# A 90-degree rotation of an 8192 x 8192 float32 matrix: the last output split into a 448-row and a 576-row part

## The chip, the cores and the metric

The kernel runs on one core of one Trainium2 chip. The metric is the device time in microseconds (us) of one execution; the median of several is given. Beside it stands a profile of one execution. Engines are named as in the profile: PE (TensorE, with PEld for its weight loads), DVE (VectorE), ACT (ScalarE), POOL (GpSimd) and SP (SyncE). SP and ACT also issue the transfers between HBM and SBUF, which 16 DMA engines carry out.

## The reference

```python
def setup_inputs():
    return {"x": np.random.randn(8192, 8192).astype(np.float32), "k": 1}

def reference(x, k):
    return np.rot90(x, k)
```

With k = 1, out[i, j] = x[j, 8191 - i]: the matrix is transposed, and the order of its columns is reversed on the way. No arithmetic is done; 268 MB are read and 268 MB are written.

## The kernel before

The matrix is cut into 16 macro blocks (`macros`) of 1024 rows (`R`) by 4096 columns (`W`), numbered `kk`. A block is read in eight loads of 128 rows by 4096 columns (2 MB; `T` = 8 loads, number `t` in the block). Each row of a load lies in a partition of its own as 16 KB. A block gives eight outputs of 2 MB (`J` = 8, number `j`), each of 512 columns of x (`CH`), that is 512 rows of the output, by 1024 columns of the output. All loads come through five buffers `buf0` to `buf4` (`LAND` + `OUTS`, 16 KB in each partition), which also hold the outputs before they are stored.

Four engines work in a chain, each with its own hand-written order.

- SP issues the loads (L160), each as soon as the buffer that it needs has been emptied (the wait at L190). At the end it waits until all stores have landed (L195).
- DVE copies each loaded buffer into `ring`, which has 63 slots of 512 columns, and reverses each 512-column chunk on the way (L209). The copy is cut into pieces where a ring slot is set free late (`pieces`, L120 to 140). The semaphore `s_rev` counts the pieces.
- PE transposes 128 x 128 blocks of `ring` by a matmul with an identity matrix into PSUM (L241). PSUM is split in two halves `ps0` and `ps1` of 2048 elements in each partition; `s_half` says that a half is full.
- ACT copies the halves into an output buffer (L272, 128 x 2048 each; `s_ev`), waits for the second one, and issues the store (L277). The store's semaphore is that of its buffer, `s_store`. Before the first half is copied, the earlier store from the same buffer must have landed (L265 to 270).

The list `outs` (L70 to 74) gives the outputs in order. Those of the first 15 blocks take one `j` and all eight `t`. The last block is taken differently: four `t` and two `j` at a time (512 columns of the output by 1024 of its rows), so the first four outputs need `t` = 0 to 3 alone; where `js` starts at 0, PE goes by `t` first (L250). The last output of all is `(15, range(4, 8), range(6, 8))`: j = 7 in the first half of PSUM, j = 6 in the second, four blocks of 128 rows each. In the store, each of the 128 partitions holds eight runs of 512 elements (2 KB), one for each block of 128 rows of the output. `out_buf` (L109) names the buffer of each output; in the last block it goes round all five.

`LINE` and `HEAD` (L28, L29) set where the buffers start in SBUF: `head` is padded so that all five start at a multiple of 1024 bytes. `whole_reads` rewrites the read side of the loads so that a row is read as one run.

The functions that the change touches, with the line numbers of the profile:

Of the kernel before, what the change touches and what calls it, by code (L numbers as in the profile page):

```python
# [6 lines left out]
P = 128  # L7
# [5 lines left out]
G = 4  # L13
J = W // (G * P)
# [3 lines left out]
CH = G * P  # L18
F = G * R
SLOTS = T * J - 1  # L20

END = T // 2

H = 2
LAND = 2
OUTS = 3

LINE = 1024  # L28
HEAD = 224  # L29


def whole_reads(nc):
# [17 lines left out]
def slot(kk, t, j):  # L50

    at = t * J + j if kk % 2 == 0 else J + t + j * T
    return (at + kk // 2 * (J + 1)) % SLOTS


def kernel(tc: tile.TileContext, x: bass.AP, k: bass.AP, out: bass.AP):
    nc = tc.nc
# [3 lines left out]
    N, M = x.shape  # L61
    dt = x.dtype
    macros = [(r0, c0) for r0 in range(0, N, R) for c0 in range(0, M, W)]
    KK = len(macros)
    n_out = KK * J
# [4 lines left out]
    outs = [(kk, range(T), [j]) for kk in range(KK - 1) for j in range(J)]  # L70
    wide = T // END
    for t in range(0, T, END):
        for j in range(0, J, wide):
            outs.append((KK - 1, range(t, t + END), range(j, j + wide)))
    assert len(outs) == n_out


    order = [(kk, a, b) for kk in range(KK) for a in range(T) for b in range(J)]
# [5 lines left out]
    with tc.tile_critical():  # L84
        head = nc.alloc_sbuf_tensor("head", [P, HEAD], dt)
        ident, scratch = head[:, :P], head[:, P : P + 1]
        bufs = [nc.alloc_sbuf_tensor(f"buf{i}", [P, F], dt) for i in range(LAND + OUTS)]
        ring = nc.alloc_sbuf_tensor("ring", [P, SLOTS * CH], dt)
        for b in bufs:
            assert nc.lookup_mloc(b).addr % LINE == 0  # L90
        ps = [
# [8 lines left out]
        s_first = nc.alloc_semaphore("s_first")  # L100
        s_half = nc.alloc_semaphore("s_half")
        s_ev = nc.alloc_semaphore("s_ev")

        def load_buf(m):
            if m < T:
# [1 line left out]
            return LAND + 2 if m == T else (m - T - 1) % LAND  # L107

        def out_buf(n):  # L109
            e = n - (n_out - J)  # L110
            if e < 0:
                return LAND + (n + 1) % OUTS
            ends = [load_buf(n_load - 2)]
            ends += [LAND + (n_out - J + i + 1) % OUTS for i in range(OUTS)]
            ends += [load_buf(n_load - 1)]
            return ends[e % len(ends)]

# [24 lines left out]
        def runs(kk, t, lo, hi):  # L142

            at = [slot(kk, t, j) for j in range(lo, hi)]
            i = 0
            while i < len(at):
                n = 1
                step = at[i + 1] - at[i] if i + 1 < len(at) else 1
                if step > 0:
                    while i + n < len(at) and at[i + n] - at[i + n - 1] == step:  # L150
                        n += 1
                else:
                    step = 1
                yield lo + i, n, at[i], step
                i += n

        def load(e, m):
            r0, c0 = macros[m // T]
            b = load_buf(m)
            e.dma_start(  # L160
                out=bufs[b][:], in_=x[r0 + m % T * P : r0 + (m % T + 1) * P, c0 : c0 + W]
            ).then_inc(s_land[b], 16)

        def uses_before(n_or_m, buf):
            return sum(buf(i) == buf(n_or_m) for i in range(n_or_m))
# [4 lines left out]
        with nc.Block() as block:  # L170

            @block.gpsimd
            def _(e):
                e.memset(ident, 0.0).then_inc(s_id, 1)  # L174
                e.wait_ge(s_id, 1)
                e.affine_select(  # L176
                    out=ident,
                    in_=ident,
                    compare_op=mybir.AluOpType.not_equal,
                    fill=1.0,  # L180
                    base=0,
                    pattern=[[-1, P]],
                    channel_multiplier=1,
                ).then_inc(s_id, 1)

            @block.sync
            def _(e):
                for m in range(LAND + OUTS, n_load):
                    last = [i for i in range(m) if load_buf(i) == load_buf(m)]
                    e.wait_ge(s_rev, rev[last[-1], J - 1])  # L190
                    load(e, m)
                for b in range(LAND + OUTS):
                    n = sum(out_buf(i) == b for i in range(n_out))
                    if n:
                        e.wait_ge(s_store[b], 16 * n)  # L195

            @block.vector
            def _(e):
                for m in range(n_load):
                    kk, t = divmod(m, T)  # L200
                    b = load_buf(m)
                    a = bufs[b][:].rearrange("p (j c) -> p j c", c=CH)
                    e.wait_ge(s_land[b], 16 * (uses_before(m, load_buf) + 1))
                    for lo, hi, wait in pieces[m]:
                        if wait:
                            e.wait_ge(*wait)
                        for j, n, at, step in runs(kk, t, lo, hi):
                            v = ring[:, at * CH : (at + (n - 1) * step + 1) * CH]
                            i = e.tensor_copy(  # L209
                                out=bass.AP(  # L210
                                    tensor=v.tensor,
                                    offset=v.offset,
                                    ap=[v.ap[0], [step * CH, n], [1, CH]],
                                ),
                                in_=a[:, j : j + n, ::-1],
                            )
                        i.then_inc(s_rev, 1)

            @block.tensor
            def _(e):  # L220
                seen = {}

                def wait(sem, n):
                    if seen.get(sem, 0) < n:
                        seen[sem] = n
                        e.wait_ge(sem, n)

                e.wait_ge(s_id, 2)
                for n, (kk, ts, js) in enumerate(outs):
                    blocks = [(j, g) for j in reversed(js) for g in range(G)]  # L230
                    half = len(blocks) // H
                    rows = len(ts) * P

                    def transpose(t, b):
                        j, g = blocks[b]
                        if n:
                            wait(s_ev, H * (n - 1) + b // half + 1)
                        wait(s_rev, rev[kk * T + t, j])
                        at = slot(kk, t, j) * CH + g * P
                        f = b % half * rows + (t - ts[0]) * P  # L240
                        i = e.transpose(  # L241
                            ps[b // half][:, f : f + P], ring[:, at : at + P], ident
                        )
                        if t == ts[-1] and b % half == half - 1:
                            i.then_inc(s_half, 1)
                        elif t == ts[0] and b == len(blocks) - 1:
                            i.then_inc(s_first, 1)

                    order = [(t, b) for b in range(len(blocks)) for t in ts]
                    if js[0] == 0:  # L250
                        order.sort()
                    for t, b in order:
                        transpose(t, b)

            @block.scalar
            def _(e):
                e.wait_ge(s_id, 2)
                e.copy(scratch, ident[:, :1])  # L258
                for n, (kk, ts, js) in enumerate(outs):
                    r0, c0 = macros[kk]  # L260
                    rows = len(ts) * P
                    b = out_buf(n)
                    for h in range(H):
                        if h == 0:
                            stores = uses_before(n, out_buf)  # L265
                            loads = [i for i in range(n_load) if load_buf(i) == b]
                            if stores:
                                e.wait_ge(s_store[b], 16 * stores)
                            elif loads:
                                e.wait_ge(s_rev, rev[loads[-1], J - 1])  # L270
                        e.wait_ge(s_half, H * n + h + 1)  # L271
                        e.copy(  # L272
                            bufs[b][:, h * F // H : (h + 1) * F // H], ps[h][:]
                        ).then_inc(s_ev, 1)
                    top = M - c0 - (js[-1] + 1) * CH
                    e.wait_ge(s_ev, H * (n + 1))
                    e.dma_start(  # L277
                        out=out[
                            top : top + len(js) * CH, r0 + ts[0] * P : r0 + ts[0] * P + rows
                        ].rearrange("(g m) f -> m g f", m=P),  # L280
                        in_=bufs[b][:].rearrange("m (g f) -> m g f", f=rows),
                    ).then_inc(s_store[b], 16)


# [33 lines left out]
```

## Time and profile before

| | |
|---|---|
| time, median of 3 runs | 1265.5 us (1265.28 to 1265.51) |
| time of the profiled execution | 1265.5 us |
| its span, first to last instruction | 1263.6 us |
| PE busy | 693.0 us (55%) |
| DVE busy | 402.9 us (32%) |
| ACT busy | 467.0 us (37%) |
| moved by DMA | 537 MB, mean 425 GB/s over the span |
| load: issue to landing, median | 16.8 us |
| store: issue to landing, median | 25.7 us |
| last store issued by ACT | at 1246.11 us, taking 1.17 us |

The span counts from the first to the last instruction of the program; the execution's own time is 1.9 us longer. "Busy" is the time in which an engine works, as a share of the span; the rows by line give the number of instructions, the mean time of one, and what ended the idle time before it. A stretch of the profile is given as start:end in us from the span's start. In its rows the DMA share is the mean busy share of the 16 DMA engines, and GB/s is what they moved. A transfer has a time of issue, on the engine that issues it, and a landing, when all of its bytes have arrived; the trace marks the end of each DMA engine's share of it apart.

### The profile page before, as it was taken

The numbers are of one execution on the slowest core, as the hardware profiler recorded it, in microseconds if no ns is written. First come the engines' busy times: TensorE is split into PE (matmuls) and PEld (weight loads), VectorE is DVE, ScalarE is ACT, GpSimd is POOL, SyncE is SP. The second block draws the span as 40 slices with busy tenths as digits, with TensorE's granted clock in tenths as the row PEclk, the third lists the DMA queues.
The fourth block names the chain that finished last, engine by engine and source line by source line (L and its number), as shares of the span: only waits on it lengthen the run. The fifth ranks groups of instructions, "written<-read, shape, count | busy, mean of one in ns | idle before, by whom it ended". The sixth has DMA issues, their size and how long they took to land.

```text
span 1263.6 us, 9359 instructions
## 1 busy us (share of the span) xinstructions
PE 693.0 (55%) x4096; PEld 647.0 (51%) x4096; DVE 402.9 (32%) x313; ACT 467.0 (37%) x258; POOL 0.7 (0%) x6
## 2 busy tenths in 40 slices
PE   1556554665545655566555555555555555556563
PEld 1445454555545545565554554555445554455563
DVE  3323432234323343322342233422234222442210
ACT  0344333433344333433334333343333433434363
POOL 0000000000000000000000000000000000000000
PEclk9987767677677776767767777777776777767787
DMA  9999999999999999999999999999999999999998
GB/s 398 415 429 429 431 426 429 428 430 429 429 428 429 429 428 429 429 428 429 428 430 428 428 429 429 429 429 428 429 429 429 429 430 427 430 429 429 428 421 338
DMA packets 36904, 537.48 MB, mean 425 GB/s; under 512 B 4096, under 2 KB 4096, under 8 KB 4096
## 3 DMA queue, kind: packets, MB, share of 16 engines
q10 hardware_dynamic: 18432, 268.44, 50.0%
q1 hardware_dynamic: 18432, 268.44, 49.8%
q8 instruction: 32, 0.52, 0.2%
q14 instruction: 8, 0.07, 0.0%
HBM read 268.44 MB, written 268.44 MB: 425 GB/s over the span
## 4 chain that ended last, share of the span: by engine, by line
DMA 80%; issue 7%; ACT 5%; DVE 5%; PE 2%; ACTq 0%; SPq 0%
DMA buf<-in_x_dram 64%; DMA out_dram<-buf 16%; ACT buf L272 5%; DVE ring L209 5%; PE ps L241 2%; ACTq L277 0%; ACTq L271 0%; SPq L313 0%; SPq L84 0%
## 5 line engine op out<-in xcount | busy, mean ns | idle before, releaser
L241 PE MATMUL ps<-head,ring 128*128 128x128 f32 x4096 | 693.0, 346 | 550.7 <-ACT buf L272 472.8
L241 PEld LDWEIGHTS ps<-head,ring 128*128 128x128 f32 x4096 | 647.0, 184 | 596.5 <-ACT buf L272 511.5
L272 ACT COPY buf<-ps 128x2048 f32<-128x2048 f32 x256 | 465.5, 1870 | 778.2 <-DMA out_dram<-buf 594.8
L209 DVE COPY ring<-buf 128x512 f32<-128x512 f32 (+7 forms) x313 | 402.9, 1336 | 812.1 <-DMA buf<-in_x_dram 811.7
L258 ACT ACT_TABLE_LOAD x1 | 1.3, 1283 | 0.9 <-SPq L84 0.9
L176 POOL TENSOR_SCALAR_AFFINE_SELECT head<-head 128x128 f32<-128x128 f32 x1 | 0.3, 293 | 0.2 <-POOL head L174 0.2
L174 POOL MEMSET head<- 128x128 f32 x1 | 0.2, 204 | 0.5 <-SPq L84 0.5
L258 ACT COPY head<-head 128x1 f32<-128x1 f32 x1 | 0.2, 191 | 0.0
L299 POOL MEMSET const-bfloat16-1.0<- 128x1 bf16 x1 | 0.1, 101 | 0.0
L299 POOL MEMSET const-uint8-127<- 128x1 uint8 x1 | 0.1, 101 | 0.0
L299 POOL MEMSET const-float32-0.0<- 128x1 f32 x1 | 0.1, 98 | 0.2 <-issue 0.2
L299 POOL MEMSET const-float32-1.0<- 128x1 f32 x1 | 0.1, 98 | 0.0
## 6 DMA issues: line engine op xcount, KB each, us to landing
buf<-in_x_dram SPq DMA_DIRECT2D x128, 2048.0 KB, 16.8
out_dram<-buf ACTq DMA_DIRECT2D x128, 2048.0 KB, 25.7
```

Of the source, the lines that this page charges most:

```text
L174: e.memset(ident, 0.0).then_inc(s_id, 1)
L176: e.affine_select(out=ident, in_=ident, compare_op=mybir.AluOpType.not_equal, fill=1.0, base=0, pattern=[[-1, P]], channel_multiplier=1,). ...
L209: i = e.tensor_copy(out=bass.AP(tensor=v.tensor, offset=v.offset, ap=[v.ap[0], [step * CH, n], [1, CH]],), in_=a[:, j : j + n, ::-1],)
L241: i = e.transpose(ps[b // half][:, f : f + P], ring[:, at : at + P], ident)
L258: e.copy(scratch, ident[:, :1])
L272: e.copy(bufs[b][:, h * F // H : (h + 1) * F // H], ps[h][:]).then_inc(s_ev, 1)
L299: nc = _bacc.Bacc("TRN2", target_bir_lowering=False, num_devices=1)
```

## The change

The last output is popped off the list and replaced by two. Rows of the output are counted from the top of the 1024 rows that the old one covered: 512 rows for j = 7, then 512 for j = 6.

- The first new output (`n_few`) holds 448 of the 512 columns of the chunk j = 7. DVE writes them into the ring slot as 16 groups of 28, each in a place of 32 columns, in an order that goes with the store. PE transposes 64 of these columns at a time, so that 28 rows of the output come to partitions 0-27 and 28 to partitions 32-59; the four partitions after each hold nothing that is stored. ACT copies two halves of 64 x 2048 as before and issues no store. SP, behind its last load, waits for the second half and issues eight stores: for each of the two partition ranges four (`SPLIT`), each of seven partitions that lie four apart, with eight runs of 512 elements in each partition. All count on a new semaphore, `s_few`.
- The second new output holds the 512 rows of j = 6 in the first half of PSUM, as before, and the remaining 64 columns of the chunk j = 7 in the second half, transposed from a new tensor `extra` (256 elements in each partition) as four blocks of 64 columns. ACT copies 128 x 2048 and 64 x 512 and issues two stores: four blocks of 128 rows, and one block of 64 rows, the latter counted on `s_few`.
- For the four loads t = 4 to 7 of the last block, DVE's piece for j = 7 becomes two copies: the 448 columns to the ring and the 64 to `extra`.
- `extra` needs room: `HEAD` shrinks from 224 to 160 and `LINE` from 1024 to 256, so that the buffers and the ring start elsewhere.
- SP's final waits take in `s_few`.

The stores and transposes of all other outputs are as they were. The core of the diff:

```diff
@@ -25,8 +25,12 @@
 
-LINE = 1024
-HEAD = 224
+FEW = 28
+SPLIT = 4
+EIGHTH = 32
+
+LINE = 256
+HEAD = 160
 
@@ -73,6 +77,21 @@
     assert len(outs) == n_out
+    kk, ts, js = outs.pop()
+    ends = [js[-1], js[0]]
+    assert len(js) == 2 and END * P * H * G == F
+    few = [(ends[0], i * 2 * FEW, FEW) for i in range(H * G)]
+    rest = [(ends[0], H * G * 2 * FEW, CH - H * G * 2 * FEW)]
+    outs.append((kk, ts, js, [few[:G], few[G:]]))
+    outs.append((kk, ts, js, [[(ends[1], g * P, P) for g in range(G)], rest]))
+    n_out += 1
+    n_few = n_out - 2
+
+    def halves(n):
+        if len(outs[n]) == 4:
+            return outs[n][3]
+        blocks = [(j, g * P, P) for j in reversed(outs[n][2]) for g in range(G)]
+        return [blocks[: len(blocks) // H], blocks[len(blocks) // H :]]
 
@@ -86,6 +105,7 @@
         ring = nc.alloc_sbuf_tensor("ring", [P, SLOTS * CH], dt)
+        extra = nc.alloc_sbuf_tensor("extra", [P, END * (CH - H * G * 2 * FEW)], dt)
         for b in bufs:
@@ -100,6 +120,7 @@
         s_ev = nc.alloc_semaphore("s_ev")
+        s_few = nc.alloc_semaphore("s_few")
 
@@ -107,11 +128,11 @@
         def out_buf(n):
-            e = n - (n_out - J)
+            e = n - (KK * J - J)
             if e < 0:
                 return LAND + (n + 1) % OUTS
             ends = [load_buf(n_load - 2)]
-            ends += [LAND + (n_out - J + i + 1) % OUTS for i in range(OUTS)]
+            ends += [LAND + (KK * J - J + i + 1) % OUTS for i in range(OUTS)]
             ends += [load_buf(n_load - 1)]
@@ -189,8 +210,28 @@
                     load(e, m)
+                kk, ts, js, _ = outs[n_few]
+                b = out_buf(n_few)
+                top = M - macros[kk][1] - (js[-1] + 1) * CH
+                left = macros[kk][0] + ts[0] * P
+                rows = len(ts) * P
+                e.wait_ge(s_ev, H * (n_few + 1))
+                for at in (0, EIGHTH):
+                    for d in range(SPLIT):
+                        first = top + at // EIGHTH * FEW + d
+                        e.dma_start(
+                            out=bass.AP(
+                                tensor=out.tensor,
+                                offset=out[first : first + 1, left : left + 1].offset,
+                                ap=[[SPLIT * M, FEW // SPLIT], [2 * FEW * M, H * G], [1, rows]],
+                            ),
+                            in_=bufs[b][at + d : at + FEW : SPLIT].rearrange(
+                                "m (g f) -> m g f", f=rows
+                            ),
+                        ).then_inc(s_few, 16)
+                e.wait_ge(s_few, 16 * (2 * SPLIT + 1))
                 for b in range(LAND + OUTS):
-                    n = sum(out_buf(i) == b for i in range(n_out))
+                    n = sum(out_buf(i) == b and i != n_few for i in range(n_out))
                     if n:
@@ -204,6 +245,21 @@
                             e.wait_ge(*wait)
+                        if kk == KK - 1 and t >= END and lo == J - 1:
+                            v = ring[:, slot(kk, t, lo) * CH :][:, :CH]
+                            i = e.tensor_copy(
+                                out=v.rearrange("p (g c) -> p g c", c=EIGHTH)[:, :, :FEW],
+                                in_=a[:, lo, CH - H * G * 2 * FEW :].rearrange(
+                                    "p (g c) -> p g c", c=FEW
+                                )[:, ::-1, ::-1],
+                            )
+                            width = CH - H * G * 2 * FEW
+                            i = e.tensor_copy(
+                                out=extra[:, (t - END) * width : (t - END + 1) * width],
+                                in_=a[:, lo, width - 1 :: -1],
+                            )
+                            i.then_inc(s_rev, 1)
+                            continue
                         for j, n, at, step in runs(kk, t, lo, hi):
@@ -226,60 +282,80 @@
                 e.wait_ge(s_id, 2)
-                for n, (kk, ts, js) in enumerate(outs):
-                    blocks = [(j, g) for j in reversed(js) for g in range(G)]
-                    half = len(blocks) // H
+                for n, (kk, ts, js, *_) in enumerate(outs):
+                    parts = halves(n)
                     rows = len(ts) * P
 
-                    def transpose(t, b):
-                        j, g = blocks[b]
+                    def transpose(t, h, b):
+                        j, off, width = parts[h][b]
                         if n:
-                            wait(s_ev, H * (n - 1) + b // half + 1)
+                            wait(s_ev, H * (n - 1) + h + 1)
                         wait(s_rev, rev[kk * T + t, j])
-                        at = slot(kk, t, j) * CH + g * P
-                        f = b % half * rows + (t - ts[0]) * P
-                        i = e.transpose(
-                            ps[b // half][:, f : f + P], ring[:, at : at + P], ident
-                        )
-                        if t == ts[-1] and b % half == half - 1:
+                        at = slot(kk, t, j) * CH + off
+                        f = b * rows + (t - ts[0]) * P
+                        v = ring[:, at : at + width]
+                        if n == n_few:
+                            width = 2 * EIGHTH
+                            at = slot(kk, t, j) * CH + b * width + h * G * width
+                            v = ring[:, at : at + width]
+                        elif n > n_few and h:
+                            at = (t - ts[0]) * width
+                            v = extra[:, at : at + width]
+                        i = e.transpose(ps[h][:width, f : f + P], v, ident)
+                        if t == ts[-1] and b == len(parts[h]) - 1:
                             i.then_inc(s_half, 1)
-                        elif t == ts[0] and b == len(blocks) - 1:
+                        elif t == ts[0] and h == H - 1 and b == len(parts[h]) - 1:
                             i.then_inc(s_first, 1)
 
-                    order = [(t, b) for b in range(len(blocks)) for t in ts]
+                    order = [
+                        (t, h, b) for h in range(H) for b in range(len(parts[h])) for t in ts
+                    ]
                     if js[0] == 0:
                         order.sort()
-                    for t, b in order:
-                        transpose(t, b)
+                    for t, h, b in order:
+                        transpose(t, h, b)
 
             @block.scalar
             def _(e):
                 e.wait_ge(s_id, 2)
                 e.copy(scratch, ident[:, :1])
-                for n, (kk, ts, js) in enumerate(outs):
+                for n, (kk, ts, js, *_) in enumerate(outs):
                     r0, c0 = macros[kk]
+                    parts = halves(n)
                     rows = len(ts) * P
                     b = out_buf(n)
                     for h in range(H):
                         if h == 0:
-                            stores = uses_before(n, out_buf)
+                            before = uses_before(n, out_buf)
                             loads = [i for i in range(n_load) if load_buf(i) == b]
-                            if stores:
-                                e.wait_ge(s_store[b], 16 * stores)
+                            if before:
+                                e.wait_ge(s_store[b], 16 * before)
                             elif loads:
                                 e.wait_ge(s_rev, rev[loads[-1], J - 1])
                         e.wait_ge(s_half, H * n + h + 1)
+                        width = 2 * EIGHTH if n == n_few else parts[h][0][2]
+                        f = len(parts[h]) * rows
                         e.copy(
-                            bufs[b][:, h * F // H : (h + 1) * F // H], ps[h][:]
+                            bufs[b][:width, h * F // H : h * F // H + f], ps[h][:width, :f]
                         ).then_inc(s_ev, 1)
+                    if n == n_few:
+                        continue
                     top = M - c0 - (js[-1] + 1) * CH
+                    col = r0 + ts[0] * P
                     e.wait_ge(s_ev, H * (n + 1))
-                    e.dma_start(
-                        out=out[
-                            top : top + len(js) * CH, r0 + ts[0] * P : r0 + ts[0] * P + rows
-                        ].rearrange("(g m) f -> m g f", m=P),
-                        in_=bufs[b][:].rearrange("m (g f) -> m g f", f=rows),
-                    ).then_inc(s_store[b], 16)
+                    stores = [(top, 0, F // rows, P)]
+                    if n > n_few:
+                        j, off, width = parts[1][0]
+                        stores = [(top + CH, 0, G, P), (top + off, G, 1, width)]
+                    for first, at, g, width in stores:
+                        e.dma_start(
+                            out=out[first : first + g * width, col : col + rows].rearrange(
+                                "(g m) f -> m g f", m=width
+                            ),
+                            in_=bufs[b][:width, at * rows : (at + g) * rows].rearrange(
+                                "m (g f) -> m g f", f=rows
+                            ),
+                        ).then_inc(s_few if g == 1 else s_store[b], 16)
 
```

## The prediction, on record before the changed kernel ran

> **What bounds the kernel now.** I read the page first. Its bars show that DMA is busy in every slice, and its queue table that nearly all of this is data.
>
> ```profile
> DMA  9999999999999999999999999999999999999998
> GB/s 398 415 429 429 431 426 429 428 430 429 429 428 429 429 428 429 429 428 429 428 430 428 428 429 429 429 429 428 429 429 429 429 430 427 430 429 429 428 421 338
> q10 hardware_dynamic: 18432, 268.44, 50.0%
> q1 hardware_dynamic: 18432, 268.44, 49.8%
> q8 instruction: 32, 0.52, 0.2%
> q14 instruction: 8, 0.07, 0.0%
> ```
>
> The reader is to see three things: the 16 DMA engines are full until the last slice (338 against 428 GB/s), loads (q1) and stores (q10) share them evenly, and two queues fetch instructions through the same engines. The time is 537 MB divided by what 16 engines carry, plus the two ends. The change touches the last output alone, so I went to the end: the stretches of its last 24 us, and the wait of SP at the program's end.
>
> ```profile
> core 0: us, PE busy (x) PEld busy (x) DVE busy (x) ACT busy (x) POOL busy (x), PEclk, DMA share, GB/s
> 1245.00:1250.00 5.00, 0.00 (x0) 0.00 (x0) 0.00 (x0) 1.08 (x1) 0.00 (x0) 0.64 1.00 419
> 1250.00:1255.00 5.00, 0.00 (x0) 0.00 (x0) 0.00 (x0) 0.00 (x0) 0.00 (x0) 0.50 0.97 406
> 1255.00:1257.00 2.00, 0.00 (x0) 0.00 (x0) 0.00 (x0) 0.00 (x0) 0.00 (x0) 0.50 0.59 246
> 1257.00:1260.00 3.00, 0.00 (x0) 0.00 (x0) 0.00 (x0) 0.00 (x0) 0.00 (x0) 0.50 0.43 180
> 1260.00:1262.00 2.00, 0.00 (x0) 0.00 (x0) 0.00 (x0) 0.00 (x0) 0.00 (x0) 0.50 0.04 16
> ...
> L195 SPq EVENT_SEMAPHORE  x2: 28/28/28, 1257.0 to 1262.0; - x2
> ```
>
> No compute engine works after 1246; stores drain until 1262.0, and not evenly: 0.97 of the engines are busy, then 0.59, 0.43, 0.04. The trace also records when each of the 16 engines marks the end of its share of a transfer. The marks of the last store (issued at 1246.11) fall at 1254.98 to 1255.12 (five), 1256.52 and 1256.91 (two), 1259.41 to 1260.38 (eight) and 1262.01 (one): **seven engines are done 5 to 7 us before the last one.** The store before it has the same pattern 4.9 to 5.0 us earlier, so this is a standing lead and no accident of the last transfer. It can be accounted for. The 32 fetches of q8 (16 KB each, taking some 1.0 us) fall on eight engines in turn: linking each packet to the one that ends where it begins, fetches 8 apart hit the same chain. Each pushes its engine back by about 1.1 us, and four of them give the 4.4 us between the five and the eight. A few 8 KB fetches of q14 (0.31 us) explain the pair. One engine has packets some ns longer than the rest all along (loads 613.6 against 611.0 ns, stores 622.5 against 618); that is the one at 1262.01.
>
> **The change, part by part.** The sum is against the profiled execution: span 1263.6, its own time 1265.5, so 1.9 us lie around the span; 1265.5 is also the median of the three runs shown. The last mark stands 1.55 us before the span's end; I keep that.
>
> *The last 2 MB, split anew.* Now every engine gets 8 packets of 16 KB of it; starts in the last stretch are 0.622 us apart, and the last marks of the last two stores (1257.02, 1262.01) give 4.98 us for the 8 packets and the mark. After the change 448 rows x 512 columns (0.92 MB) go in eight transfers of seven partitions, 56 packets of 16 KB as long as one partition makes one packet, as it does now. I take one packet of each transfer for each of seven engines: 8 x (0.622 + 0.009 for the 4-byte mark) = 5.05 us for these seven, nothing for the other nine. All 16 get the rest: 8 packets of 8 KB (four blocks of 128 rows) and 4 of 2 KB (the 64 rows). No row has such packets. By bytes they take 8 x 0.311 + 4 x 0.078 + 2 marks = 2.82 us; a fixed cost like the 9 ns of a 4-byte packet on each of the 12 makes it 2.93; I take 2.82, as 16 KB packets of four runs (615 ns) and of eight (626) show that pieces cost little.
> So the nine lose 4.98 - 2.82 = **2.16 us** and the seven gain 5.05 + 2.82 - 4.98 = **2.89 us**. New last marks: the slow engine 1262.01 - 2.16 = 1259.85; the eight 1260.38 - 2.16 = 1258.22; the seven, if they are those with the lead, 1256.91 + 2.89 = 1259.80 at most. The end moves to 1259.85: -2.16.
>
> The price of the seven-engine assignment hangs on something that no row of before shows: each of its transfers has 16 marks. [...]
>
> *SP.* Eight issues come behind the loads, after a wait for the second half's copy (1246.1). Nothing is behind them but the final waits. A load's issue takes 0.33 us (0.53 at most), so 2.6 to 4.2 us; at ACT's longest (1.17) 9.4 us, to 1255.5. Hidden: the seven still have the store before (marks 1250.0 to 1251.9) in hand, and then their 2.8 us of the rest. Without that cover each us of delay beyond it would be one of the end.
>
> *ACT and PE.* ACT drops one issue (1.17) and adds a 128x2048 copy (1.87) and a 64x512 one (191 ns for one column and 1870 for 2048 give 0.61). PE adds 20 transposes at 3.73/32 = 0.117, 2.3 us, partly beside the copies. From 1246.07 ACT waits for 16 transposes begun when the first half was free (1244.26 + 1.87 = 1246.13), copies to 1248.7 and issues twice (0.55 each, 1.17 at worst) by 1251.0. The nine have the store before until 1254.4 or later: hidden by 3 us. The new output's buffer was last stored in a transfer landed by 1242.14, so its wait costs nothing.
>
> *DVE.* In four loads a 128x512 copy (0.418) becomes two: zero to 0.42 us more each. DVE idles 7.2 us before each load, and its last piece ends at 1215.0, while these columns are transposed from 1239.97: nothing.
>
> *Instruction fetch.* PE's stream grows by 40 instructions. Fetches come every 256, four outputs of 64; the last was at 1239.8, and a further one would need some 250 more: none. SP's added instructions may bring its next 8 KB fetch (one stands at 1265.4, behind the span) forward: 0 or 0.31 us, on one engine.
>
> *Moved buffers.* The five buffers now start at a multiple of 256 bytes instead of 1024. No row shows what that does to a packet. All 2048 data packets of an engine would pay: 1 ns is 2.05 us. Between loads of one run (611) and stores of eight (626) lie 15 ns, so the ends are -31 and +31 us; I take 0, as run length, not address, is what differs between these rows, and give the rest to a rival.
>
> Sum: 1265.5 - 2.16 = 1263.34, plus some 0.1 for fixed costs of small packets: **1263.4**. Its own range: 0.31 for an early fetch, 0.31 if the 64-partition transfer runs at half pace, and 0.3 the other way: 1262.7 to 1264.2.
>
> **Rivals.**
> - *The slow engine is among the seven.* [...] Price: 1262.01 + 2.89, so +2.9: **1268.4**, slower. It decides as soon as the engine of the last mark carries more than 8 packets' worth of the last 2 MB.
> - *The seven are among the eight that fetch.* 1260.38 + 2.89 = 1263.27, +1.3: **1266.8**. [...]
> - *The transfers spread over all engines.* 56 packets / 16 = 3.5 each, 2.2 + 2.8 us, as now: **1265.5**; the change then does not do what it says. [...] Only the marks of the new transfers can tell.
> - *Moved buffers slow the stream.* From 1.3 ns a packet on it eats the gain and 0.1% more; at 2 ns, 1263.4 + 4.1 = **1267.5**.
>
> **How the numbers follow.** About 0.2% (2.5 us) is what a measurement of this kernel can tell from no change, and the forecast of -2.1 lies inside it. Forecast 0.56 (0.10 of it beyond 2.5 us); slow engine among the seven 0.13; fetching engines 0.10; spread 0.07; buffers 0.08 (0.06 slower, 0.02 faster); others 0.06, such as all 56 packets on one engine (56 x 0.622, some 30 us more), 0.03 of it faster. Faster 0.10 + 0.02 + 0.03 = 0.15; slower 0.13 + 0.06 + 0.03 = 0.22; within 0.63. The range takes in the forecast, the spread, the fetching and the slow engine: 1262.7 to 1268.5.
>
> **What would show it.** The seven-partition transfers have seven late marks each and nine at once; the last marks of all engines lie within 2 us, at about 1259.8, and the GB/s of the last slice rises. Packets of loads and stores keep 611 and 615 ns in the middle. Wrong if the last mark belongs to a seven-partition transfer and is later than 1262, or if the pace in mid-span changes.

## The result, and the profile after

The changed kernel takes 1268.09 us (median of 14 runs, 1267.79 to 1268.38) beside 1265.36 us of the kernel before (14 runs): a ratio of 1.0021, 95% interval 1.0014 to 1.0028. It is 2.7 us slower, where 2.1 us faster was forecast; 1268.4 was the price of the first rival, that the slow DMA engine is among the seven.

The page of the changed kernel, bars and queue table:

```profile
DMA  9999999999999999999999999999999999999997
GB/s 398 419 429 430 428 428 430 428 430 428 429 429 430 429 429 429 428 428 430 428 430 428 429 429 430 429 429 429 428 430 428 430 429 428 430 429 428 429 418 308
q1 hardware_dynamic: 18544, 269.36, 49.9%
q10 hardware_dynamic: 18512, 267.53, 49.8%
q8 instruction: 32, 0.52, 0.2%
q14 instruction: 8, 0.07, 0.0%
```

The middle of the span is the same stream as before. The last slice has fallen from 338 to 308 GB/s, so the time is lost at the very end. The 0.92 MB have moved from ACT's queue (q10) to SP's (q1), and PE's fetches (q8) are still 32. The stretches of the end:

```profile
core 0: us, PE busy (x) PEld busy (x) DVE busy (x) ACT busy (x) POOL busy (x), PEclk, DMA share, GB/s
1250.00:1255.00 5.00, 0.00 (x0) 0.00 (x0) 0.00 (x0) 0.71 (x2) 0.00 (x0) 0.65 0.94 390
1255.00:1257.00 2.00, 0.00 (x0) 0.00 (x0) 0.00 (x0) 0.00 (x0) 0.00 (x0) 0.50 0.79 321
1257.00:1260.00 3.00, 0.00 (x0) 0.00 (x0) 0.00 (x0) 0.00 (x0) 0.00 (x0) 0.50 0.38 158
1260.00:1262.00 2.00, 0.00 (x0) 0.00 (x0) 0.00 (x0) 0.00 (x0) 0.00 (x0) 0.50 0.17 71
1262.00:1264.50 2.50, 0.00 (x0) 0.00 (x0) 0.00 (x0) 0.00 (x0) 0.00 (x0) 0.50 0.06 22
```

And SP's eight new issues, with their durations in ns (least, median, most) and the start of the first and the last:

```profile
L222 SPq DMA_DIRECT2D out_dram<-buf x8: 787/1086/1424, 1248.0 to 1255.6; - x8
```

Between 1260 and 1262, 0.17 of the DMA engines are busy: three of sixteen. After 1262.2 it is one. Which they are, the packets of the trace tell, linked into chains as in the prediction (each to the one that ends where it begins; a chain is one engine's work): the 56 packets of the seven-partition transfers lie on seven chains. Four of these belong to the lead (the seven engines that were early before), two to the fetching engines (the eight that carry PE's fetches), and one is the slow engine (the one with longer packets). The nine others have no such packet. The two fetching engines end at 1262.2 and the slow one at 1264.0, with its last mark at 1264.48; before, the slow one's was 1262.01. Four of its eight 16 KB packets (0.626 us each) lie between those of the last whole store. Behind that store come the other four, among eight of 8 KB (0.315 us), and then four of 2 KB (0.084 us).

So the transfers did go to seven fixed engines, eight packets each, as the change means them to. They were not the seven that are early.

### The profile page after: what moved, and what is told of

It is laid out like the page before. It is cut to its first block, busy times and chain, and to the rows that moved or that the text cites. A ratio compares the mean times of both kernels' runs of the same rounds, so it can differ in the third digit from the quotient of the medians.

```text
span 1266.0 us, 9416 instructions
## 1 busy us (share of the span) xinstructions
PE 719.2 (57%) x4116; PEld 675.2 (53%) x4116; DVE 403.3 (32%) x317; ACT 469.4 (37%) x260; POOL 0.7 (0%) x6
## 4 chain that ended last, share of the span: by engine, by line
DMA 79%; issue 8%; DVE 5%; ACT 4%; PE 2%; ACTq 0%; SPq 0%
DMA buf<-in_x_dram 69%; DMA out_dram<-buf 10%; DVE ring L265 5%; ACT buf L338 4%; PE ps L304 2%; ACTq L351 0%; SPq L181 0%; ACTq L335 0%; SPq L389 0%; SPq L103 0%
## 5 line engine op out<-in xcount | busy, mean ns | idle before, releaser
L304 PE MATMUL ps<-head,ring 128*128 128x128 f32 (+1 forms) x4112 | 718.8, 354 | 529.5 <-ACT buf L338 462.1
L304 PEld LDWEIGHTS ps<-head,ring 128*128 128x128 f32 (+1 forms) x4112 | 674.8, 189 | 573.2 <-ACT buf L338 497.0
L338 ACT COPY buf<-ps 128x2048 f32<-128x2048 f32 (+1 forms) x258 | 468.0, 1866 | 780.4 <-DMA out_dram<-buf 602.3
```

Source lines behind the costliest of these rows:

```text
L304: i = e.transpose(ps[h][:width, f : f + P], v, ident)
L338: e.copy(bufs[b][:width, h * F // H : h * F // H + f], ps[h][:width, :f]).then_inc(s_ev, 1)
```

## The experiments

The theory after the result, **theory 1**: the slow engine is among the seven and pays the whole +2.9 us; everything else in the sum holds. **Theory 2**: the moved buffers lengthen the packets. **Theory 3**: SP's eight issues (9.0 us in all) set the end.

**The layout alone.** The kernel before with these lines (the code cuts of this section show the main lines of each edit; ... stands for what is left out)

```diff
-LINE = 1024
-HEAD = 224
+LINE = 256
+HEAD = 160
+        extra = nc.alloc_sbuf_tensor("extra", [P, END * 64], dt)
```

> The kernel before with the changed layout alone: HEAD 160, LINE 256, and the tensor extra allocated but unused; every transfer is as before. Theory 1 (the slow engine is among the seven and pays 2.9 us): no difference, 1265.4 within 0.3, packets of 611 and 615 ns. Theory 2 (moved buffers slow the stream by about 1.3 ns a packet): 1268 and longer packets.

Measured 1265.27 us beside 1265.40, ratio 1.0001 (0.9992 to 1.0010). Between 200 and 1200 us loads take 611.6 ns and stores 615.7 on average, as before (611.6 and 615.6). Theory 2 falls.

This trace shows one thing more: the lead of the early engines is no fixed quantity. All seven early marks of the last store fall at 1257.27 to 1257.44 here, 2.2 us ahead of the eight (1259.61 to 1260.53) and 4.8 ahead of the slow one (1262.20), where the kernel before had 4.3 us and more between the first five and the eight. The same stretch in the kernel before, here, and in the changed kernel:

```profile
1234.00:1238.00 4.00, 3.43 (x31) 3.15 (x30) 0.00 (x0) 3.38 (x2) 0.00 (x0) 1.00 1.05 438
1234.00:1238.00 4.00, 3.73 (x32) 3.46 (x32) 0.00 (x0) 3.33 (x2) 0.00 (x0) 1.00 0.88 369
1234.00:1238.00 4.00, 3.43 (x32) 3.14 (x31) 0.00 (x0) 3.33 (x3) 0.00 (x0) 1.00 0.87 365
```

In the second and third the DMA engines are only 0.88 and 0.87 busy. In the layout run it is the seven early chains that stand still: their packets end at 1235.6 to 1236.7, and all seven go on at 1237.0 to 1237.2, with the next store. So the seven lost part of their lead where they stood still until the next store: it is 2.2 us here. In the changed kernel the seven then mark its last whole store at 1251.63 to 1251.79, 2.8 us before the first fetching engine (1254.58). The slow engine sets the end in the layout run too, so the time does not show this.

**Which engines, first try.** In the kernel before, the last store but two leaves SP in pieces:

```diff
+STEPS = list(range(15, 1, -1)) + [9]
...
+                for k in STEPS:
+                    e.dma_start(
+                        out=to[p : p + k],
+                        in_=bufs[b][p : p + k].rearrange("m (g f) -> m g f", f=rows),
+                    ).then_inc(s_few, 16)
+                    p += k
```

> The kernel before, but its last store but two (2 MB, 128 partitions) goes from SP in transfers of 15, 14, ... 2 and 9 partitions instead of one from ACT. If a transfer of k partitions takes the k lowest-numbered engines, engine 0 and 1 get 15 packets of it, 2 gets 14, then 13, 12, 11, 10, 9 (engine 7), 8, 6, 5, 4, 3, 2, 1 and engine 15 none, so that the count on each chain of packets names its engine. Theory 1: the chain that ends last has between 9 and 15 of these packets. If it is engine 0 or 1, 7 packets more than before: 1265.4 + 4.4 = 1269.8; engine 6, 2 more: 1266.7. [...] If transfers do not take the lowest engines, all chains count 6 to 10 and the time stays.

Measured 1274.74 us (ratio 1.0074, 1.0060 to 1.0088): later than theory 1 had it (1269.8 at most). 59 of the 128 packets took more than 0.7 us, up to 3.66, so the time says nothing of the count. The slow chain, the one that ends last, carries 12 of them; that is engine 4, if each transfer of k partitions takes the first k engines of one order, as the expectation supposes.

**Fewer issues.** The changed kernel with two transfers of 28 partitions in place of eight of seven:

```diff
-                    for d in range(SPLIT):
...
-                            in_=bufs[b][at + d : at + FEW : SPLIT].rearrange(
...
+                        in_=bufs[b][at : at + FEW].rearrange("m (g f) -> m g f", f=rows),
```

> The changed kernel, but the 448 rows leave SP in two transfers of 28 partitions instead of eight of seven. [...] Theory 2 (layout): stays at 1268.

Measured 1267.10 us (1.0014, 1.0005 to 1.0023). Theory 2 had 1268. Theory 1 gives 1268.1 - 4 x 0.631 = 1265.6, if the slow engine has four of the packets in place of eight; that it has four is not shown. Theory 3, with two issues in place of eight, gives the forecast of 1263.4. 25 of the 56 packets took more than 0.7 us, up to 1.99; in the changed kernel one did, with 0.702. The 28 partitions lie side by side, which may have brought in a second effect, so this run settles nothing on the count; the next ones keep the partitions four apart.

**Which engines, with partitions four apart.** The kernel before, with part of its last store but two sent in seven steps:

```diff
+STEPS = [(0, 8), (1, 7), (2, 6), (3, 5), (32, 4), (33, 3), (34, 2)]
...
+                for p, k in STEPS:
+                    e.dma_start(
+                        out=to[p : p + 4 * k - 3 : 4],
```

> The kernel before, but of its last store but two only 35 of 128 partitions are stored, in seven transfers of 8, 7, 6, 5, 4, 3 and 2 partitions that lie four apart (from partitions 0, 1, 2, 3, 32, 33, 34); 93 partitions of that output are left out. If k partitions take the k lowest-numbered engines, engines 0 and 1 get 7 of these packets, 2 gets 6, 3 five, 4 four, 5 three, 6 two, 7 one and the others none. The pace of a chain before it (lead, fetching, slow) then has a number. Theory 1: the slow chain counts 2 to 7, two fetching ones and four of the lead are among the seven. Rival (the slow engine is 7 or above): it counts 1 or 0. If the steps of four are what kept packets at 0.62 us, these stay under 0.7 us where those of contiguous partitions took up to 3.6.

Read from its trace alone (one run, in which most of that output is not stored, so that its time says nothing here). The packets stay at 0.63 us on average (most 0.70). The slow chain, whose last mark (1259.02) comes 2.4 us after the next one, counts 4: by the same count engine 4 again. Three other late chains carry 3, 2 and 1 marks of these transfers, as engines 5 to 7 would. The early chains ran dry in this run and started again together, so that their links are not clean; but most of the packets lie on them. The reading is: engines 0 to 3 in the lead, 4 slow, 5 and 6 fetching. It gives four, one and two for the seven of the change, as its own trace shows. These numbers are places in the supposed order, with which the counts agree; that they are the numbering of the chip, no trace shows. The lead of 0 to 3 is put to the test further down.

**Half of the transfers, and none.** The changed kernel with `for at in (0,)` (224 rows not stored), and with `for at in ()` (448 rows not stored).

> The changed kernel with the first four of its eight seven-partition transfers alone; the other 224 rows are not stored. Theory 1 (the slow engine pays 0.631 us for each): 1268.1 - 4 x 0.631 = 1265.6. Theory 3 (SP's eight issues of about 1.1 us set the end): 4.5 us less, 1263.6. Theory of moved work that is hidden: no change, 1268.1.

> The changed kernel without its eight seven-partition transfers; 448 rows are not stored, all the rest is as in the changed kernel. Theory 1: the slow engine has 2.82 us after its last whole store instead of 7.87, so 1268.1 - 5.05 = 1263.1, which is also what the gain on the other nine engines was to be. Rival (the 8 KB and 2 KB packets of the rest cost more than their bytes): above 1264.

Measured 1265.76 us (10 runs) and 1263.19 us (10 runs; ratio 0.9981, 0.9972 to 0.9990). From 1268.09 these are steps of 2.33 and 2.57 us for four transfers each; 4 x 0.631 = 2.52 was expected. The last stretches of the kernel without the transfers:

```profile
core 0: us, PE busy (x) PEld busy (x) DVE busy (x) ACT busy (x) POOL busy (x), PEclk, DMA share, GB/s
1255.00:1257.00 2.00, 0.00 (x0) 0.00 (x0) 0.00 (x0) 0.00 (x0) 0.00 (x0) 0.50 0.55 229
1257.00:1260.00 3.00, 0.00 (x0) 0.00 (x0) 0.00 (x0) 0.00 (x0) 0.00 (x0) 0.50 0.11 44
1260.00:1262.00 2.00, 0.00 (x0) 0.00 (x0) 0.00 (x0) 0.00 (x0) 0.00 (x0) 0.50 0.00 0
```

No data moves after 1260. The slow engine's last mark is 1259.82, 2.83 us after that of the last whole store (1256.99); 2.82 was worked out. Theory 3 is not needed, and the first step speaks against it: dropping four of the eight issues was to give 4.5 us and gave 2.33.

**Only the lead.** If this reading holds, transfers of four partitions go to engines 0 to 3 alone, and these are early. The changed kernel with `FEW = 16`: 256 columns go that way, and the other 256 as two blocks of 128 rows. The ring slot is laid out in quarters, so that `extra` is not needed:

```diff
-FEW = 28
+FEW = 16
...
-    rest = [(ends[0], H * G * 2 * FEW, CH - H * G * 2 * FEW)]
+    rest = [(ends[0], H * G * 2 * FEW + q * P, P) for q in range(2)]
...
+                            at = slot(kk, t, j) * CH + h * G + b
+                            v = ring[:, at : at + 8 * width - 7 : 8]
...
-                        stores = [(top + CH, 0, G, P), (top + off, G, 1, width)]
+                        stores = [(top + CH, 0, G, P), (top + off, G, 2, width)]
```

> The changed kernel with transfers of four partitions instead of seven: 256 of the 512 columns are transposed into partitions 0-15 and 32-47 and stored in eight transfers of four partitions that lie four apart; the other 256 go with the rest as two blocks of 128 rows. Theory 1, with engine 4 as the slow one and engines 0 to 3 in the lead (from the counts of the stepped run): the slow engine has 8 x 0.314 + 8 x 0.157 + marks = 3.8 us after its last whole store instead of 4.98, the four 5.05 + 3.8 = 8.85 from 1250.0 to 1251.9, that is 1260.8 at most. The end moves by -1.2 against before: 1264.2. Rival (the classes are numbered otherwise, and a fetching or slow engine is among the four): 5.05 - 1.2 more on that one, 1267.5 to 1269.3.

> The kernel with transfers of four partitions once more, to narrow its interval against the kernel before. Theory 1: 1264.2 to 1264.5 beside 1265.4, with the marks of the slow engine and of the four within 0.5 us of each other at 1260.5. Rival (its gain was chance): 1265.4.

Measured 1264.54 us beside 1265.42 (ratio 0.9994, 0.9985 to 1.0003), and in the second set 1264.34 beside 1265.46 (0.9991, 0.9982 to 1.0000); 1264.2 had been worked out. Either interval still touches 1. In the second set all 11 runs (1264.12 to 1264.59) lie under all 15 of the kernel before (1264.98 to 1266.13). Against the changed kernel it is 3.5 to 3.8 us less. The stretches of the first of the two:

```profile
core 0: us, PE busy (x) PEld busy (x) DVE busy (x) ACT busy (x) POOL busy (x), PEclk, DMA share, GB/s
1255.00:1257.00 2.00, 0.00 (x0) 0.00 (x0) 0.00 (x0) 0.00 (x0) 0.00 (x0) 0.50 0.84 348
1257.00:1260.00 3.00, 0.00 (x0) 0.00 (x0) 0.00 (x0) 0.00 (x0) 0.00 (x0) 0.50 0.42 169
1260.00:1262.00 2.00, 0.00 (x0) 0.00 (x0) 0.00 (x0) 0.00 (x0) 0.00 (x0) 0.50 0.00 0
```

All engines stop by 1260.6 (last marks 1260.43, 1260.50, 1260.55), and 0.84 instead of 0.59 of them are busy from 1255 to 1257. The slow chain carries none of the 32 new packets. That is the picture that was forecast for the change itself.

**Side by side or four apart.** The changed kernel, with each transfer's seven partitions next to each other; the number of packets and the bytes are the same.

```diff
-                        first = top + at // EIGHTH * FEW + d
+                        n = FEW // SPLIT
+                        first = top + at // EIGHTH * FEW + d * n
...
-                            in_=bufs[b][at + d : at + FEW : SPLIT].rearrange(
+                            in_=bufs[b][at + d * n : at + (d + 1) * n].rearrange(
```

> The changed kernel, but each of the eight transfers takes seven partitions that lie side by side instead of four apart; engines, packets and bytes are the same. Theory A (only the count of packets on the slow engine matters): 1268.1. Theory B (packets of engines that read neighbouring partitions at once get in each other's way, as the packets of 0.9 to 2.0 us in the run with 28 partitions suggest): those packets are longer than 0.7 us and the time is 1270 or more.

Measured 1271.24 us (1.0046, 1.0032 to 1.0061). SP's issues in it:

```profile
L223 SPq DMA_DIRECT2D out_dram<-buf x8: 956/2423/2982, 1246.4 to 1260.4; - x8
```

And the stretches of its end:

```profile
1260.00:1262.00 2.00, 0.00 (x0) 0.00 (x0) 0.00 (x0) 0.00 (x0) 0.00 (x0) 0.50 0.43 103
1262.00:1264.50 2.50, 0.00 (x0) 0.00 (x0) 0.00 (x0) 0.00 (x0) 0.00 (x0) 0.50 0.37 85
```

Read the share against the rate. In the changed kernel 0.17 of the engines moved 71 GB/s; here 0.43 move 103. The packets are longer for the same bytes: 1.04 us on average and 2.63 at most, against 0.624 and 0.702. What theory B forecast came (packets over 0.7 us, a time above 1270), and it accounts for the miss of the run with 28 partitions in kind. The cause that it names, packets in each other's way, no trace shows. SP's last issue ends only at 1263.3 here, and the last of these packets begins at 1267.3; how much of the 3.15 us comes from the longer packets directly and how much through the later issues, the run does not separate.

## Why the prediction was wrong, point by point

- **What bounds the kernel: right.** The DMA engines are 0.94 busy from 1250 to 1255, and the end is set by the one engine with longer packets (last mark 1264.48). Taking the transfers away, and with them one packet each from that engine, moved the time by 0.58 and 0.64 us for each (2.33 / 4 and 2.57 / 4).
- **The step that failed**, in the prediction's words: "the seven, if they are those with the lead". Seven marks are early and seven engines are used, and I let the equal numbers stand for equal engines. The runs show the seven to be four of the lead (0 to 3), the slow one (4) and two fetching ones (5 and 6). By the sum the slow engine so gained 2.89 us of work instead of losing 2.16; in the trace its last mark moved from 1262.01 to 1264.48, by 2.47 us.
- **Which seven engines.** That a transfer of seven partitions uses seven engines, and that the slow one is not among them, the trace of before does not show: it has no engine numbers, and each of its transfers has 16 marks. The trace of the changed kernel shows the first (56 packets on seven chains, eight on each) and refutes the second. The first k engines of one order agree with the runs: 12 and 4 packets on the slow chain in two sets of steps (recorded on two chips, 0 and 2), both of them engine 4 by that count, and four-partition transfers, none of whose 32 packets is on the slow chain, with 1264.54 us beside 1265.42. The one sign that the trace of before gave for the slow engine, that its chain is the first to start (at 1.96 us), was taken for a low place in such an order, and the rival was given 0.13.
- **A standing lead: right in order, wrong as a fixed amount.** The first five were 4.3 us and more ahead of the eight in the trace of before; in the layout run all seven were 2.2 us ahead, in the changed kernel 2.8. With the marks of the layout run the same sum would have put the early seven at 1257.44 + 2.89 = 1260.33, behind the slow engine at 1262.20 - 2.16 = 1260.04, and would have forecast a gain of 1.9 us.
- **The sum: right in its sizes.** +2.9 for the slow engine among the seven against +2.7 measured; -2.16 without the transfers against 1263.19 - 1265.51 = -2.3 us; 0.315 and 0.084 us for the 8 KB and 2 KB packets against 0.311 and 0.078.
- **SP's issues: wrong in size, right in effect.** 0.79 to 1.42 us each instead of 0.33 to 0.53, 9.0 us in all. They end at 1257.05, while the slow engine works on packets at hand until 1264.0.
- **DVE, PE, ACT, fetches: right.** DVE's two copies take 0.38 and 0.19 us and end at 1214.6; PE has no 33rd fetch; ACT's new copy takes 0.58 (0.61 estimated), and its last two issues begin at 1250.7 and 1251.3.
- **Moved buffers: right**, at nothing: 1265.27 us beside 1265.40 in the layout run.
- **The other rivals.** The seven all among the fetching engines: wrong, two are. Spread over all engines: wrong, nine chains have no such packet.
- **The range** of 1262.7 to 1268.5 takes in 1268.09 because that rival was counted into it; the direction was wrong.

## What to carry to other kernels

Here the DMA engines were busy to the end and stopped at different times (seven marks at 1254.98 to 1256.91, the last at 1262.01), and the number of partitions of a transfer moved work between them: transfers of four put none of their 32 packets on the slow engine (1264.54 us beside 1265.42), transfers of seven put eight of their 56 on it (1268.09 beside 1265.36). In such a case find out first which engines are early: here transfers of 8, 7, 6, ... 2 partitions, four apart, in one profiled run told them by count (4 on the slow chain). Two groups of the same size are no proof that they are the same group. A few early engines are worth only what the latest one gives up (2.3 us here, without the transfers), so see that it is not among those that take the load.

## What the runs showed of the hardware

- In these runs transfers with few partitions did better with the partitions apart. In transfers of seven partitions four apart, a 16 KB packet took 0.624 us; with seven neighbouring partitions it took 1.04 on average and up to 2.63. Why neighbouring ones took longer, no run shows.
- A DMA issue of SP took 0.33 us for a 2 MB load and 0.79 to 1.42 us for 112 KB at the end of the program; in the run with neighbouring partitions, up to 2.98. What the issue waits for was not tried.
- The 32 instruction fetches of q8, one for every four outputs and so taken for PE's, take time of the DMA engines that carry the data: 16 KB and 1.0 us each. By the linked chains they fall on eight engines in turn. That they make the 4.3 us between those eight and the first five in the kernel before is argued from 4 x 1.1 us and not tried; with the same 32 fetches the distance was 2.2 us in the layout run. Why one engine has longer packets (in the kernel before, loads of 613.6 ns against 611.0 and stores of 622.5 against 618) was not tried either.
